# Instance norm over rows of 4096: two of four rows' statistics move to batch-norm instructions and to ScalarE

## The chip, the cores and the metric

The kernel runs on one core of one Trainium2 chip. The metric is the device time of one execution in microseconds (us), input and output in HBM. Lower is better.

## The reference

For each of 256 x 256 = 65,536 rows of 4096 numbers, the mean is taken off and the result is divided by the standard deviation:

```python
x = np.random.randn(256, 256, 4096).astype(np.float32)
eps = np.float32(1e-5)

mean = np.mean(x, axis=2, keepdims=True)
var = np.var(x, axis=2, keepdims=True)
return ((x - mean) / np.sqrt(var + eps)).astype(np.float32)
```

The input is 1073.74 MB and so is the output; each number is read once and written once.

## The kernel before

**Tiles.** The 65,536 rows are cut into 128 tiles. A tile has 128 partitions, and each partition holds K = 4 rows of d = 4096 fp32 numbers, so a tile is 8.39 MB. It lies in one of BUFS = 3 buffers `X[s]` in SBUF and is normalised in place there. One load brings a tile and one store takes it away.

**Order.** Each engine has its program written out by hand, and semaphores tie the programs together. SP issues all loads and stores, from one queue: `store(t)` waits for five counts of `done[s]` and then issues (L157); the `load(t + 2)` that follows in the program waits until `store(t - 1)`, the last from the same buffer, has landed, and then issues (L162). At the start three loads are issued at once. GpSimd only waits for the last stores. On VectorE and ScalarE one tile is handled after the other, in a loop over three tiles (one for each buffer) with a few tiles written out at both ends.

**VectorE**, in `vector_tile`, waits for the load, then

1. sums each of the four rows (`reduce_sum`, L83), and counts `means` up after each;
2. for two rows at a time: waits for ScalarE's roots (`stds`), takes the reciprocal (L91), multiplies it with the negative mean (L93), and normalises the rows in place with `tensor_scalar` (L105), x * rstd + nbias. Of the fourth row it does the last quarter alone, from Q = 3072 on.

**ScalarE**, in `scalar_tile`, follows row by row: when a row's sum is there it takes a Square pass over (sum - d * x) with an accumulated output (L129), which yields the row's squared deviations in `ss`; the squares themselves go to `junk` in PSUM and are never read. After two rows it takes the root of both with one small instruction (L138). At the end of the tile it waits for `scaled` and normalises the first three quarters of the fourth row with an Identity pass (L143).

The waits on an engine's own semaphore (`own_v`, `own_a`) come before an instruction that reads what the engine has just written. `take` waits for a count and clears the semaphore (L67).

Of the kernel before, what the change touches and what calls it, by code (L numbers as in the profile page):

```python
# [9 lines left out]
@with_exitstack  # L10
def kernel(
    ctx: ExitStack,
    tc: tile.TileContext,
    x: bass.AP,
    eps: bass.AP,
    out: bass.AP,
):
    nc = tc.nc
    fp32 = mybir.dt.float32
    AX = mybir.AxisListType  # L20
    AF = mybir.ActivationFunctionType
    ALU = mybir.AluOpType
    P = 128
    K = 4
    BUFS = 3
    Q = 3072

    x_flat = x.flatten_outer_dims()
    out_flat = out.flatten_outer_dims()
    n, d = x_flat.shape  # L30
    assert n % (P * K) == 0 and d & (d - 1) == 0

    ntiles = n // (P * K)
    x_t = x_flat.rearrange("(t p k) d -> t p k d", p=P, k=K)
    out_t = out_flat.rearrange("(t p k) d -> t p k d", p=P, k=K)
    assert ntiles == 128

    pool = ctx.enter_context(tc.tile_pool(name="pool", bufs=1))
    psum = ctx.enter_context(tc.tile_pool(name="psum", bufs=1, space=bass.MemoryType.PSUM))


    eps_tile = pool.tile([P, 1], fp32)

    junk = psum.tile([P, d], fp32)
    X = [pool.tile([P, K, d], fp32, name=f"x{s}") for s in range(BUFS)]
    total, ss, std, rstd, nbias = (
        [pool.tile([P, K], fp32, name=f"{name}{s}") for s in range(BUFS)]
        for name in ("total", "ss", "std", "rstd", "nbias")
    )

    loaded = [nc.alloc_semaphore(f"loaded{s}") for s in range(BUFS)]
    stored = [nc.alloc_semaphore(f"stored{s}") for s in range(BUFS)]
    own_v = nc.alloc_semaphore("own_v")
    own_a = nc.alloc_semaphore("own_a")
    means = nc.alloc_semaphore("means")
    stds = nc.alloc_semaphore("stds")
    scaled = nc.alloc_semaphore("scaled")  # L60
    done = [nc.alloc_semaphore(f"done{s}") for s in range(BUFS)]
    ready = nc.alloc_semaphore("ready")
    issued = nc.alloc_semaphore("issued")

    def take(engine, sem, count):
        engine.wait_ge(sem, count)
        engine.sem_clear(sem)  # L67

    V, A, S, G = nc.vector, nc.scalar, nc.sync, nc.gpsimd

    def vector_tile(s):

        x = X[s]
        own = 0

        def mine(instruction):
            nonlocal own
            own += 1
            return instruction.then_inc(own_v, 1)

        take(V, loaded[s], 16)
        for r in range(K):
            V.reduce_sum(out=total[s][:, r : r + 1], in_=x[:, r, :], axis=AX.X).then_inc(means, 1)  # L83
        for b in range(0, K, 2):
            c = slice(b, b + 2)
            final = b == K - 2
            if final:
                take(V, stds, b // 2 + 1)
            else:
                V.wait_ge(stds, b // 2 + 1)  # L90
            mine(V.reciprocal(out=rstd[s][:, c], in_=std[s][:, c]))  # L91
            V.wait_ge(own_v, own)
            mine(V.scalar_tensor_tensor(  # L93
                out=nbias[s][:, c], in0=total[s][:, c], scalar=-1.0 / d, in1=rstd[s][:, c], op0=ALU.mult, op1=ALU.mult
            ))
            if final:
                take(V, own_v, own)
            else:
                V.wait_ge(own_v, own)
            if final:  # L100
                V.sem_inc(scaled, 1)
            for r in range(b, b + 2):
                c = slice(r, r + 1)
                f = slice(Q, d) if r == K - 1 else slice(0, d)
                V.tensor_scalar(  # L105
                    out=x[:, r, f], in0=x[:, r, f], scalar1=rstd[s][:, c], scalar2=nbias[s][:, c],
                    op0=ALU.mult, op1=ALU.add,
                ).then_inc(done[s], 1)

    def scalar_tile(s):  # L110

        x = X[s]
        last = K - 1
        own = 0

        def mine(instruction):
            nonlocal own
            own += 1
            return instruction.then_inc(own_a, 1)

        for r in range(K):
            c = slice(r, r + 1)
            if own:
                A.wait_ge(own_a, own)
            if r == last:
                take(A, means, K)
            else:
                A.wait_ge(means, r + 1)
            mine(A.activation(  # L129
                out=junk, in_=x[:, r, :], func=AF.Square, bias=total[s][:, c], scale=-float(d), accum_out=ss[s][:, c]  # L130
            ))
            if r % 2:
                c = slice(r - 1, r + 1)
                if r == last:
                    take(A, own_a, own)
                else:
                    A.wait_ge(own_a, own)
                A.activation(  # L138
                    out=std[s][:, c], in_=ss[s][:, c], func=AF.Sqrt, bias=eps_tile, scale=1.0 / d**3
                ).then_inc(stds, 1)  # L140
        c = slice(last, last + 1)
        take(A, scaled, 1)
        A.activation(  # L143
            out=x[:, last, :Q], in_=x[:, last, :Q], func=AF.Identity, bias=nbias[s][:, c], scale=rstd[s][:, c]
        ).then_inc(done[s], 1)

    def rows_of(ap, t):

        if isinstance(t, int):
            return ap[t]  # L150
        first, period, count, i = t
        ap = ap[first : first + period * (count - 1) + 1 : period]
        return ap[bass.ds(i, 1)].rearrange("o p k d -> p (o k) d")

    def store(s, t):
        take(S, done[s], K + 1)
        S.dma_start(out=rows_of(out_t, t), in_=X[s][:, :, :]).then_inc(stored[s], 16)  # L157

    def load(s, t, wait=True):
        if wait:  # L160
            take(S, stored[s], 16)
        S.dma_start(out=X[s][:, :, :], in_=rows_of(x_t, t)).then_inc(loaded[s], 16)  # L162

    last = ntiles - 1
    rounds = (ntiles - 5) // BUFS
    L0 = 2

    with tc.tile_critical():  # L168
        for t in range(BUFS):
            load(t, t, wait=False)  # L170
        store(0, 0)
        store(1, 1)
        load(0, 3)

        with S.Fori(0, rounds) as i:
            for t in range(L0, L0 + BUFS):
                store(t % BUFS, (t, BUFS, rounds, i))
                load((t + 2) % BUFS, (t + 2, BUFS, rounds, i))
        load(last % BUFS, last)
        store((last - 2) % BUFS, last - 2)  # L180
        store((last - 1) % BUFS, last - 1)
        store(last % BUFS, last)
        S.sem_inc(issued, 1)
        take(G, issued, 1)
        for s in range(BUFS):
            take(G, stored[s], 16)

        V.memset(eps_tile, eps).then_inc(ready, 1)  # L188
        vector_tile(0)
        vector_tile(1)  # L190
        with V.Fori(0, rounds) as i:  # L191
            for j in range(BUFS):
                vector_tile((L0 + j) % BUFS)
        vector_tile((last - 2) % BUFS)
        vector_tile((last - 1) % BUFS)
        vector_tile(last % BUFS)

        take(A, ready, 1)
        scalar_tile(0)
        scalar_tile(1)  # L200
        with A.Fori(0, rounds) as i:
            for j in range(BUFS):
                scalar_tile((L0 + j) % BUFS)
        scalar_tile((last - 2) % BUFS)
        scalar_tile((last - 1) % BUFS)
        scalar_tile(last % BUFS)
# [35 lines left out]
```

## Time and profile before

| | us |
|---|---|
| median of three runs | 4962.89 |
| lowest and highest | 4960.41, 4966.53 |
| the profiled execution, its own time | 4962.78 |
| its span, first to last instruction | 4961.0 |
| VectorE busy, 1537 instructions | 3293.7 (66%) |
| ScalarE busy, 1410 instructions | 2401.5 (48%) |
| bytes moved by DMA | 2147.52 MB, mean 433 GB/s |
| load, from issue to landing, median | 50.4 |
| store, from issue to landing, median | 31.6 |

The page and the trace come from one profiled execution. DVE stands for VectorE, ACT for ScalarE, POOL for GpSimd, SP for SyncE; a "q" behind a name is that engine's sequencer. L12 is line 12 of the kernel. The page cuts the span into 40 equal slices and gives each engine's busy share as a digit, in tenths; 9 is 90% or more. Under it stands the mean share of the 16 DMA engines and what they moved. A group of instructions has its line, engine and operation, then output<-input with shapes and the number of instructions; after the first bar the busy time in us and the mean of one in ns, after the second the engine's idle time ahead of them and what ended most of it. A row of the waits reads: who waited for whom, us in all, how many times, the longest. A row of the timeline has the start, the duration, then the group, and in brackets the idle time ahead of it. Several instructions with one name are merged there; "x4 17.40" is four instructions from the first one's start to the last one's end. SP's rows are transfers being issued, not moved.

### The profile page before, as it was taken

How to read it: one execution, taken by the hardware profiler on the slowest of the kernel's cores; microseconds unless marked ns; L12 is line 12 of the kernel's file. 1: busy time of each engine (PE TensorE's matmuls, PEld its weight loads, DVE VectorE, ACT ScalarE, POOL GpSimd, SP SyncE). 2: the span in 40 equal slices, each digit the busy share in tenths (PEclk: the TensorE clock that was granted, in tenths of full speed). 3: DMA queues.
4: the chain of work that ended last, by engine and by line, in shares of the span. 5: the costliest groups of instructions: out<-in, count | busy, mean ns of one | idle time of the engine just before them, and what ended most of it. 6: DMA issues, size and time to landing. Idle time of an engine off the chain costs nothing.

```text
span 4961.0 us, 5413 instructions
## 1 busy us (share of the span) xinstructions
DVE 3293.7 (66%) x1537; ACT 2401.5 (48%) x1410; POOL 0.2 (0%) x4
## 2 busy tenths in 40 slices
DVE  6666666666666666666666666666666666666666
ACT  4454444554445544554445544455444554445544
POOL 0000000000000000000000000000000000000000
DMA  9999999999999999999999999999999999999999
GB/s 423 431 430 435 432 434 435 432 434 436 433 432 438 431 434 435 433 433 436 432 433 434 435 431 434 437 432 433 435 433 433 437 431 434 433 435 432 435 435 414
DMA packets 36866, 2147.52 MB, mean 433 GB/s; under 512 B 4096, under 2 KB 4096, under 8 KB 4096
## 3 DMA queue, kind: packets, MB, share of 16 engines
q1 hardware_dynamic: 36864, 2147.50, 100.0%
q14 instruction: 2, 0.02, 0.0%
HBM read 1073.74 MB, written 1073.74 MB: 433 GB/s over the span
## 4 chain that ended last, share of the span: by engine, by line
DVE 62%; another core or an unknown queue 31%; issue 4%; DMA 2%; DVEq 0%; SPq 0%
DVE total L83 44%; DVE x L105 17%; DMA x<-in_x_dram 1%; DVE nbias L93 1%; DMA out_dram<-x 1%; DVE rstd L91 1%; DVEq L67 0%; DVEq L191 0%; SPq L67 0%; SPq L237 0%; SPq L168 0%
## 5 line engine op out<-in xcount | busy, mean ns | idle before, releaser
L83 DVE TENSOR_REDUCE total<-x 128x1 f32<-128x4096 f32 x512 | 2226.9, 4412 | 1597.4 <-DMA x<-in_x_dram 1597.4
L129 ACT ACTIVATE junk<-x,total 128x4096 f32<-128x4096 f32 x512 | 1882.9, 3678 | 2368.4 <-DVE total L83 2368.3
L105 DVE TENSOR_SCALAR x<-x,rstd,nbias 128x4096 f32<-128x4096 f32 (+1 forms) x512 | 1007.3, 2009 | 33.6 <-DVE nbias L93 28.9
L143 ACT ACTIVATE x<-x,nbias,rstd 128x3072 f32<-128x3072 f32 x128 | 377.3, 2948 | 144.3 <-DVEq L67 144.3
L129 ACT ACTIVATION_READ_ACCUMULATOR junk<-x,total 128x1 f32 x512 | 95.4, 186 | 0.0
L138 ACT ACTIVATE std<-ss,eps_tile 128x2 f32<-128x2 f32 x256 | 75.6, 295 | 19.0
L93 DVE SCALAR_TENSOR_TENSOR nbias<-total,rstd 128x2 f32<-128x2 f32 x256 | 41.0, 160 | 8.9
L91 DVE RECIPROCAL rstd<-std 128x2 f32<-128x2 f32 x256 | 39.8, 156 | 0.0
L129 ACT ACT_TABLE_LOAD x1 | 1.3, 1283 | 1.2 <-DVE eps_tile L188 1.2
L138 ACT ACT_TABLE_LOAD x1 | 1.3, 1283 | 0.0
L188 DVE MEMSET eps_tile<- 128x1 f32 x1 | 0.1, 59 | 1.0 <-SPq L168 1.0
L223 POOL MEMSET const-bfloat16-1.0<- 128x1 bf16 x1 | 0.1, 102 | 0.0
L223 POOL MEMSET const-uint8-127<- 128x1 uint8 x1 | 0.1, 102 | 0.0
L223 POOL MEMSET const-float32-0.0<- 128x1 f32 x1 | 0.1, 99 | 0.2 <-issue 0.2
L223 POOL MEMSET const-float32-1.0<- 128x1 f32 x1 | 0.1, 99 | 0.0
## 6 DMA issues: line engine op xcount, KB each, us to landing
x<-in_x_dram SPq DMA_DIRECT2D x128, 50.4
out_dram<-x SPq DMA_DIRECT2D x128, 31.6
```

Source lines behind the costliest of these rows:

```text
L83: V.reduce_sum(out=total[s][:, r : r + 1], in_=x[:, r, :], axis=AX.X).then_inc(means, 1)
L91: mine(V.reciprocal(out=rstd[s][:, c], in_=std[s][:, c]))
L93: mine(V.scalar_tensor_tensor(out=nbias[s][:, c], in0=total[s][:, c], scalar=-1.0 / d, in1=rstd[s][:, c], op0=ALU.mult, op1=ALU.mult))
L105: V.tensor_scalar(out=x[:, r, f], in0=x[:, r, f], scalar1=rstd[s][:, c], scalar2=nbias[s][:, c], op0=ALU.mult, op1=ALU.add,).then_inc(done ...
L129: mine(A.activation(out=junk, in_=x[:, r, :], func=AF.Square, bias=total[s][:, c], scale=-float(d), accum_out=ss[s][:, c]))
L138: A.activation(out=std[s][:, c], in_=ss[s][:, c], func=AF.Sqrt, bias=eps_tile, scale=1.0 / d**3).then_inc(stds, 1)
L143: A.activation(out=x[:, last, :Q], in_=x[:, last, :Q], func=AF.Identity, bias=nbias[s][:, c], scale=rstd[s][:, c]).then_inc(done[s], 1)
L188: V.memset(eps_tile, eps).then_inc(ready, 1)
L223: nc = _bacc.Bacc("TRN2", target_bir_lowering=False, num_devices=1)
```

## The change

The four rows of a tile are no longer treated alike.

- **Rows 0 and 1**: VectorE sums them as before, ScalarE takes the Square pass.
- **Row 2**: VectorE takes batch-norm statistics in chunks of `F = BN_STATS_FMAX` elements (`bn_stats`) and joins them to mean and variance (`bn_aggr`). ScalarE takes only the root of that variance.
- **Row 3**: ScalarE takes the sum, in an Identity pass with accumulated output, and then the Square pass. A new semaphore `started`, which VectorE counts up when the load has landed, lets ScalarE begin with it at once.
- **Normalising**: VectorE does row 3, row 1 and the first three quarters of row 2; ScalarE does row 0 and the last quarter of row 2. It was three and a quarter rows and three quarters of a row.
- The columns of the small tiles are rotated by one (`column(r)`), so that rows 3 and 0 lie side by side and share a reciprocal and a root. Roots come in three counts of `stds` for a tile instead of two, `means` in three instead of four, `scaled` in two instead of one. `done` stays at five.
- Loads, stores, their order, SP's and GpSimd's programs, tile size and number of buffers stay as they are.

The core of the diff, the unchanged helpers left out:

```diff
+    F = nc.vector.BN_STATS_FMAX
+    chunks = d // F
+    stats = pool.tile([P, chunks, nc.vector.BN_STATS_DIM], fp32)
+    mv = [pool.tile([P, nc.vector.BN_AGGR_DIM], fp32, name=f"mv{s}") for s in range(BUFS)]
+    started = nc.alloc_semaphore("started")
+    def column(r):
+        return (r + 1) % K
...
         take(V, loaded[s], 16)
-        for r in range(K):
-            V.reduce_sum(out=total[s][:, r : r + 1], in_=x[:, r, :], axis=AX.X).then_inc(means, 1)
...
+        V.sem_inc(started, 1)
+        sum_of(0)
+        sum_of(1)
+        for f in range(chunks):
+            part = V.bn_stats(out=stats[:, f, :], in_=x[:, 2, f * F : (f + 1) * F])
+        mine(part)
+        settle()
+        V.bn_aggr(out=mv[s], in_=stats).then_inc(means, 1)
+        V.wait_ge(stds, 1)
+        scales(columns(3, 0))
+        V.sem_inc(scaled, 1)
+        normalise(3, slice(0, d))
+        take(V, stds, 3)
+        c, e = columns(1), columns(2)
+        mine(V.reciprocal(out=rstd[s][:, columns(1, 2)], in_=std[s][:, columns(1, 2)]))
+        settle()
+        mine(V.scalar_tensor_tensor(
+            out=nbias[s][:, c], in0=total[s][:, c], scalar=-1.0 / d, in1=rstd[s][:, c], op0=ALU.mult, op1=ALU.mult
+        ))
+        mine(V.scalar_tensor_tensor(
+            out=nbias[s][:, e], in0=mv[s][:, 0:1], scalar=-1.0, in1=rstd[s][:, e], op0=ALU.mult, op1=ALU.mult
+        ))
+        settle(True)
+        V.sem_inc(scaled, 1)
+        normalise(1, slice(0, d))
+        normalise(2, slice(0, Q))
...
+        take(A, started, 1)
+        mine(A.activation(out=junk, in_=x[:, K - 1, :], func=AF.Identity, accum_out=total[s][:, columns(K - 1)]))
+        A.wait_ge(own_a, own)
+        square(K - 1)
+        A.wait_ge(own_a, own)
+        A.wait_ge(means, 1)
+        square(0)
+        root(columns(3, 0))
+        A.wait_ge(means, 2)
+        square(1)
+        root(columns(1), True)
+        take(A, means, 3)
         A.activation(
-            out=x[:, last, :Q], in_=x[:, last, :Q], func=AF.Identity, bias=nbias[s][:, c], scale=rstd[s][:, c]
-        ).then_inc(done[s], 1)
+            out=std[s][:, columns(2)], in_=mv[s][:, 1:2], func=AF.Sqrt, bias=eps_tile, scale=1.0
+        ).then_inc(stds, 1)
+        A.wait_ge(scaled, 1)
+        normalise(0, slice(0, d))
+        take(A, scaled, 2)
+        normalise(2, slice(Q, d))
```

In the new code `settle` is the wait on `own_v`, `scales` the reciprocal with its multiply, and `normalise` the `tensor_scalar` on VectorE and the Identity pass on ScalarE.

## The prediction

> **What bounds the kernel now.** I read the slices first, because an average can hide a stage; then the DMA section, then the waits, and only then the chain. The page's slices:
>
> ```profile
> DVE  6666666666666666666666666666666666666666
> ACT  4454444554445544554445544455444554445544
> ...
> DMA  9999999999999999999999999999999999999999
> GB/s 423 431 430 435 432 434 435 432 434 436 433 432 438 431 434 435 433 433 436 432 433 434 435 431 434 437 432 433 435 433 433 437 431 434 433 435 432 435 435 414
> ...
> q1 hardware_dynamic: 36864, 2147.50, 100.0%
> ```
>
> VectorE is busy for six tenths of every slice, ScalarE for four or five, and the 16 DMA engines for all of each. The transfers move 431 to 438 GB/s everywhere but in the first slice and the last. There is one queue, filled by SP alone, and what moves (each element in once, out once) is not touched by the change. The waits say the same:
>
> ```profile
> DVE total L83 <- DMA x<-in_x_dram: 1597.4, 125, 21.9
> ```
>
> VectorE spends 1597 us waiting for loads: 125 waits, 12.8 us each. The chain of waits looks different, and here it misleads:
>
> ```profile
> DVE 62%; another core or an unknown queue 31%; issue 4%; DMA 2%; DVEq 0%; SPq 0%
> ```
>
> It is walked back through semaphores: a store was issued because VectorE finished, so VectorE's work gets the blame. The walk does not show that the store, once issued, stood in line behind a load already in the queue. One tile from the middle of the timeline settles that (VectorE and SP; start, duration):
>
> ```profile
> 2406.53 17.40 DVE L83 TENSOR_REDUCE total<-x 128x1 f32<-128x4096 f32 x4 [12.70 <-DMA x<-in_x_dram]
> ...
> 2429.42 3.13 DVE L105 TENSOR_SCALAR x<-x,rstd,nbias 128x4096 f32<-128x4096 f32 x2 [0.19 <-DVE nbias L93]
> ...
> 2432.80 0.34 SPq L157 DMA_DIRECT2D out_dram<-x  x1
> 2433.38 0.35 SPq L162 DMA_DIRECT2D x<-in_x_dram  x1
> 2445.31 17.40 DVE L83 TENSOR_REDUCE total<-x 128x1 f32<-128x4096 f32 x4 [12.76 <-DMA x<-in_x_dram]
> ```
>
> The tile lands at 2406.53 and its store is issued at 2432.80, 26.27 us later. The load of the next tile is still running then and lands at 2445.31. So the store has **12.5 us of cover**: it could come that much later before the DMA engines had nothing to do, and coming earlier only makes it wait longer. Landings are 2445.31 - 2406.53 = 38.78 us apart here; a load and a store of 8.39 MB each at 434 GB/s take 38.66. The period is the transfers' and nothing else.
>
> [...] of the 65,536-byte packets, the median is 2.418 us both where VectorE is busy throughout and where it is idle. So another mix of instructions should not change the rate.
>
> **The change, part by part.** The profiled execution took 4962.78 us, 1.78 around its span of 4961.0; the median of the runs is 4962.89, practically the same. Durations come from these rows:
>
> ```profile
> L83 DVE TENSOR_REDUCE total<-x 128x1 f32<-128x4096 f32 x512 | 2226.9, 4412 | 1597.4 <-DMA x<-in_x_dram 1597.4
> L129 ACT ACTIVATE junk<-x,total 128x4096 f32<-128x4096 f32 x512 | 1882.9, 3678 | 2368.4 <-DVE total L83 2368.3
> L105 DVE TENSOR_SCALAR x<-x,rstd,nbias 128x4096 f32<-128x4096 f32 x384 | 914.8, 2410 | 33.6 <-DVE nbias L93 28.9
> L143 ACT ACTIVATE x<-x,nbias,rstd 128x3072 f32<-128x3072 f32 x128 | 377.3, 2948 | 144.3 <-DVEq L67 144.3
> L105 DVE TENSOR_SCALAR x<-x,rstd,nbias 128x1024 f32<-128x1024 f32 x128 | 103.3, 807 | 0.0
> ```
>
> I follow one tile from its landing (time 0).
>
> VectorE before: 17.40 for four sums (4.33 from start to start), 0.4 to 0.7 of waits and small instructions twice, 4.74 for two rows of normalising, 3.13 for one and a quarter: 26.3.
>
> VectorE after: two sums end at 8.74. The bn_stats (I take the chunk BN_STATS_FMAX as 512 elements, so eight; no view shows it) have no row. [...] 0.69 us each, 5.5 us for eight, an estimate. [...] Ceiling that I allow: twice the estimate, 11. bn_aggr over 8 triples with its wait: 0.2 to 1, I take 0.45. That is 14.7. Reciprocal and multiply (0.156 + 0.160 and the gaps between, 0.4): 15.1. Row 3, 2.41: 17.5. Three small instructions with two waits, 0.8: 18.3. Row 1, 2.37: 20.7. 3072 elements of row 2, interpolated between 807 and 2410 ns, 1.87: **22.5**.
>
> ScalarE after: it starts on the landing, with an Identity pass that sums row 3, at the price of a Square pass (3.68 + 0.19, 3.90 from start to start), then three Squares: 11.7 after the third pass, a root 12.1, the fourth pass 16.0, two roots 16.7. By then the sums (4.4, 8.7) and the aggregate (14.7) are there. Then Identity over row 0, 2.95 plus 1024 elements [...]: 3.8, to 20.5; and a quarter of row 2, 1.2: 21.7. [...]
>
> So the store would be issued at about 22.7 instead of 26.3, **3.6 us earlier**, and its cover grows from 12.5 to 16.1 us. All added work lies beside the transfers, which hide it: value on the path 0. If that cover were gone, the 3.6 us per tile would come through in full.
>
> The new waits: ScalarE now waits for "started" at the head of a tile; nothing is queued behind it but the next tile's work, and VectorE gives it on the landing. VectorE's wait for three roots comes at 17.5, after they are done (16.7). If a wait were late by a microsecond or two, VectorE's last rows and then SP's store would be late by as much, against 16 us of cover. SP's and POOL's programs are unchanged: the same 256 transfers in the same order, five counts per store as before. A load needs the store before the last to have landed; that store was issued near 2394 (38.7 before) and landed about 31.6 later, near 2426, so issuing at about 2429 still finds it done.
>
> **The two ends.** In front: the first store is issued at 49.18, while the third load runs until about 61.6; moved to 45.5 it starts no sooner. At the back: the last store is issued at 4934.63 and stands behind the one before, which by the trace's landing events is complete at 4939.6; issued some 7 us earlier, it still stands behind it. The windows agree (us; VectorE, ScalarE and POOL busy with counts; clock; DMA share; GB/s):
>
> ```profile
> 4920.00:4940.00 20.00, 14.26 (x10) 12.31 (x9) 0.00 (x0) 1.00 1.00 433
> 4940.00:4961.00 21.00, 0.00 (x0) 0.00 (x0) 0.00 (x0) 1.00 0.77 334
> ```
>
> The DMA engines are full to 4940 and then drain; the 0.77 is their emptying at different times, up to the last store's end. Sum: 4962.78 + 0 = 4963; I say 4962.5.
>
> **The rivals.** *Faster, the chain is right:* 3.6 us x 128 = 460 us, 4500 us. Against it stands the queue, full in every slice; at 434 GB/s the 2147.5 MB alone take 4948. What could still come is the removal of small hindrances: landings are on average 38.70 us apart over the middle tiles and 38.59 at the least, from some late packets; 0.11 x 124 = 13 us if all vanished, 4949. Nothing ties them to the old order. Chance 0.04 of more than 0.2%.
>
> *Slower, bn_stats makes VectorE the bound:* its work per tile is on the path once it passes 38.65 us, so once the eight take 5.5 + 16.1 = 21.6 us, 2.7 each, four times my estimate. At five times (3.45 each) a tile is 44.6 us, and 128 x 44.6 + 23 for the first load + 20 for the last store = 5750. No row of before excludes it[...]. Chance 0.03, all slower cases together.
>
> *The change does not do what it says:* the sums could end no earlier because ScalarE is late, leaving the store at 26. The time is the same 4962, so this tells on the trace alone and belongs to no change.
>
> **How the numbers follow.** No change, within 0.2% (10 us, about what a measurement of this kernel can tell from none): 0.93. The three runs lie between 4960.4 and 4966.5; a little more on both sides, for late packets and another few runs, gives 4957 to 4968. The two rivals lie outside with 0.07 together, so the range needs no stretching to them.
>
> **What would show it.** Right: DMA at 9 in all slices near 434 GB/s, VectorE and ScalarE at five tenths or a little more, VectorE's waits for loads up from 12.8 to about 16 us each, store to landing up from 31.6 to about 35, bn_stats near 0.7 us. Wrong: slices with less DMA, VectorE without waits for loads, bn_stats over 2.7 us, or packets whose median leaves 2.418 us.

## The result, and the profile after

The changed kernel takes **4970.27 us** (median of 15 executions, 4968.99 to 4975.68); the kernel before, measured beside it, 4961.23 (15 executions, 4959.56 to 4966.53). The ratio is **1.0018, with a 95% interval of 1.0010 to 1.0025**: slower by 9 us. That is still within the 0.2% that the prediction called no change, but above the top of its range (4968), and the interval does not reach 1.

What the change was to do on the engines, it did. Groups of instructions of the kernel after (busy us, mean ns, idle time ahead), and the wait of VectorE for loads:

```profile
L99 DVE TENSOR_REDUCE total<-x 128x1 f32<-128x4096 f32 x256 | 1119.4, 4414 | 2189.5 <-DMA x<-in_x_dram 2189.5
L121 DVE BATCH_NORM_STATS2 stats<-x 128x6 f32<-128x512 f32 x1024 | 618.9, 678 | 0.0
L124 DVE BATCH_NORM_AGGREGATE mv<-stats 128x2 f32<-128x48 f32 x128 | 47.5, 371 | 4.4
```

```profile
DVE total L99 <- DMA x<-in_x_dram: 2189.5, 125, 32.9
```

A bn_stats over 512 elements takes 678 ns, an aggregate 371, and VectorE waits 2189.5 / 125 = 17.5 us for each load, where it was 12.8. One tile from the middle of the timeline (start, duration; VectorE and SP):

```profile
2408.32 8.75 DVE L99 TENSOR_REDUCE total<-x 128x1 f32<-128x4096 f32 x2 [17.40 <-DMA x<-in_x_dram]
...
2416.98 4.83 DVE L121 BATCH_NORM_STATS2 stats<-x 128x6 f32<-128x512 f32 x8
...
2425.52 4.20 DVE L111 TENSOR_SCALAR x<-x,rstd,nbias 128x4096 f32<-128x4096 f32 x2 [0.19 <-DVE nbias L136]
2429.97 0.34 SPq L205 DMA_DIRECT2D out_dram<-x  x1
2430.55 0.35 SPq L210 DMA_DIRECT2D x<-in_x_dram  x1
2447.09 8.74 DVE L99 TENSOR_REDUCE total<-x 128x1 f32<-128x4096 f32 x2 [17.36 <-DMA x<-in_x_dram]
```

The store is issued 21.65 us after the landing instead of 26.27, and its cover, the time until the load ahead of it has landed, is 17.1 us (2447.09 - 2429.97) instead of 12.5. All this is gain, and all of it is hidden. The loss is in the transfers. The slices of the kernel after:

```profile
DMA  9999999999999999999999999999999999999998
GB/s 422 433 433 433 435 433 436 431 436 433 432 437 432 435 433 432 436 432 435 434 432 436 433 434 434 432 437 432 436 433 433 436 432 436 432 434 435 433 437 380
```

In 39 slices nothing is to be seen; the last has 380 GB/s, where it had 414. The windows of the end show what that is (us; busy time of VectorE, ScalarE and POOL; clock; DMA share; GB/s). First the kernel before, then the one after:

```profile
4950.00:4955.00 5.00, 0.00 (x0) 0.00 (x0) 0.00 (x0) 1.00 0.97 419
4955.00:4961.00 6.00, 0.00 (x0) 0.00 (x0) 0.00 (x0) 1.00 0.13 55
```

```profile
4950.00:4955.00 5.00, 0.00 (x0) 0.00 (x0) 0.00 (x0) 1.00 0.76 328
4955.00:4960.00 5.00, 0.00 (x0) 0.00 (x0) 0.00 (x0) 1.00 0.09 39
4960.00:4965.00 5.00, 0.00 (x0) 0.00 (x0) 0.00 (x0) 1.00 0.06 26
```

A share of 0.06 is 1/16: from 4960 to 4965 **one DMA engine works alone**, at 26 GB/s, while the packets of the other 15 have ended by 4957.4. Before, the share is 0.97 up to 4955, and the last packet of all ends at 4959.5; after, at 4967.1.

That engine had not stopped anywhere. A transfer adds 16 counts to its semaphore (the trace has 4096 for 256 transfers), and there are 16 DMA engines. Each count comes some 0.36 us behind the end of a 4-byte packet, of which there are 4096 too. I take it that each engine gives one, so that the time from the first count to the last is how far the engines have drifted apart. From the trace's landing events, in us, for the landings number 20 to 254 of 256:

```
landing                      20    60   100   140   180   220   254
before                      2.9   4.0   3.7   3.7   4.1   3.5   4.5
after                       3.7   4.1   5.4   7.8  10.2  12.6  14.5
```

Before, the spread settles near 4 us. After, one engine falls back steadily, by 0.12 us a tile. The trace's packet records show how. There are 32,768 packets of 65,536 bytes for 256 transfers and 16 engines, eight for each engine and tile, with a median of 2.418 us. In the middle of the run after, the packets of the other engines have that duration to within 3 ns, but for a few late ones; those of the last engine take longer, a little in each (ns over 2418, means over the 15 stores and 15 loads among landings 150 to 180):

```
the eight packets of a store   10.7  4.1  1.0  6.5 13.9 21.6 34.7 24.5    sum 117
the eight packets of a load     0.9  0.2  4.0  1.9  4.9  2.0  5.6  2.0    sum  21
```

Five sixths are lost in stores, which this engine moves during the first 19.3 us after a landing, and most of it from 9 us on, when bn_stats, roots and normalising run. The kernel before has the same at a smaller size: one engine, the last one from about landing 222 on, loses 52 ns in a store and 23 in a load. The question of the experiments was therefore: what of the change reaches one DMA engine?

### The profile page after: what moved, and what is told of

Its sections match the earlier page's. It is cut to its first block, busy times and chain, and to the rows that moved or that the text cites. A ratio compares the mean times of both kernels' runs of the same rounds, so it can differ in the third digit from the quotient of the medians.

```text
span 4968.7 us, 6565 instructions
## 1 busy us (share of the span) xinstructions
DVE 2684.0 (54%) x2433; ACT 2639.5 (53%) x1666; POOL 0.2 (0%) x4
## 2 busy tenths in 40 slices
DMA packets 36867, 2147.52 MB, mean 432 GB/s; under 512 B 4096, under 2 KB 4096, under 8 KB 4096
## 4 chain that ended last, share of the span: by engine, by line
DVE 50%; another core or an unknown queue 43%; issue 4%; DMA 2%; ACT 0%; DVEq 0%; SPq 0%; ACTq 0%
DVE total L99 22%; DVE x L111 13%; DVE stats L121 12%; DMA x<-in_x_dram 1%; DVE mv L124 1%; DMA out_dram<-x 1%; DVE nbias L104 0%; DVE rstd L131 0%; DVE nbias L133 0%; DVE nbias L136 0%; DVEq L72 0%; ACT junk L156 0%; DVE rstd L102 0%; ACT junk L176 0%
## 5 line engine op out<-in xcount | busy, mean ns | idle before, releaser
L99 DVE TENSOR_REDUCE total<-x 128x1 f32<-128x4096 f32 x256 | 1119.4, 4414 | 2189.5 <-DMA x<-in_x_dram 2189.5
L176 ACT ACTIVATE junk<-x 128x4096 f32<-128x4096 f32 x128 | 459.1, 3587 | 2241.9 <-DVEq L72 2241.9
L156 ACT ACTIVATE junk<-x,total 128x4096 f32<-128x4096 f32 x384 | 1409.9, 3672 | 8.3
L111 DVE TENSOR_SCALAR x<-x,rstd,nbias 128x4096 f32<-128x4096 f32 (+1 forms) x384 | 846.5, 2232 | 43.2 <-DVE nbias L136 23.9
L171 ACT ACTIVATE x<-x,nbias,rstd 128x4096 f32<-128x4096 f32 (+1 forms) x256 | 629.6, 2506 | 0.0
L121 DVE BATCH_NORM_STATS2 stats<-x 128x6 f32<-128x512 f32 x1024 | 618.9, 678 | 0.0
L165 ACT ACTIVATE std<-ss,eps_tile 128x2 f32<-128x2 f32 (+1 forms) x256 | 75.5, 295 | 19.0
L124 DVE BATCH_NORM_AGGREGATE mv<-stats 128x2 f32<-128x48 f32 x128 | 47.5, 371 | 4.4
L187 ACT ACTIVATE std<-mv,eps_tile 128x1 f32<-128x1 f32 x128 | 35.7, 279 | 0.0
L176 ACT ACTIVATION_READ_ACCUMULATOR junk<-x 128x1 f32 x128 | 23.9, 186 | 0.0
L176 ACT ACT_TABLE_LOAD x1 | 1.3, 1283 | 23.1 <-DVEq L72 23.1
L165 ACT ACT_TABLE_LOAD x1 | 1.3, 1283 | 0.0
## 6 DMA issues: line engine op xcount, KB each, us to landing
out_dram<-x SPq DMA_DIRECT2D x128, 36.4
```

Of the source, the lines that this page charges most:

```text
L99: V.reduce_sum(out=total[s][:, columns(r)], in_=x[:, r, :], axis=AX.X).then_inc(means, 1)
L111: V.tensor_scalar(out=x[:, r, f], in0=x[:, r, f], scalar1=rstd[s][:, c], scalar2=nbias[s][:, c], op0=ALU.mult, op1=ALU.add,).then_inc(done ...
L121: part = V.bn_stats(out=stats[:, f, :], in_=x[:, 2, f * F : (f + 1) * F])
L124: V.bn_aggr(out=mv[s], in_=stats).then_inc(means, 1)
L156: mine(A.activation(out=junk, in_=x[:, r, :], func=AF.Square, bias=total[s][:, c], scale=-float(d), accum_out=ss[s][:, c]))
L165: A.activation(out=std[s][:, c], in_=ss[s][:, c], func=AF.Sqrt, bias=eps_tile, scale=1.0 / d**3).then_inc(stds, 1)
```

## The experiments

Each was timed against the kernel before on the same chip; the kernel before had medians of 4960.8 to 4961.1 in all four groups. "Lost per store" is the sum over the eight packets of the engine that falls behind, a mean over the stores in which that engine is clearly the last one (by 40 ns or more) and none of its packets is late by 90 ns or more. In the kernel before these are ten stores near the end.

### First group: bn_stats, the number of instructions, or the earlier store?

**e1_bn_added**: the kernel before with

```diff
             V.reduce_sum(out=total[s][:, r : r + 1], in_=x[:, r, :], axis=AX.X).then_inc(means, 1)
+        for f in range(d // F):
+            V.bn_stats(out=spare[:, f, :], in_=x[:, 2, f * F : (f + 1) * F])
```

> The kernel before, plus eight bn_stats over row 2 on VectorE after the four sums of each tile; what they write is not used. The changed kernel was 9 us slower and its trace ends with one DMA engine working alone for some 8 us. Theory A (each VectorE instruction that is fetched takes about 10 ns of one of the 16 DMA engines, whatever it does): eight more per tile, 8 x 10 ns x 128 = 10 us, about 4971 us, and in the trace one DMA engine alone at the end (DMA share 0.06). Theory B (bn_stats alone disturbs a DMA engine): about 4971 us as well. Theory C (the earlier store or ScalarE's new order is the cause): no change, 4961 us, since both are as before here.

Measured: 5010.15 us (4973 to 5027), ratio 1.0091 (1.0061 to 1.0122). Far more than any of the theories said.

**e2_sums_added**: the same place and count with another operation.

```diff
+        for f in range(d // F):
+            V.reduce_sum(out=spare[:, f : f + 1], in_=x[:, 2, f * F : (f + 1) * F], axis=AX.X)
```

> The kernel before, plus eight reduce_sum of 512 elements each over row 2 after the four sums of each tile; their output is not used. The same count, operand and length as eight bn_stats. Theory A (the count of VectorE's instructions): about 4971 us and one DMA engine alone at the end. Theory B (bn_stats alone): 4961 us. Theory C (earlier store or ScalarE's order): 4961 us.

Measured: 4995.54 us (4973 to 5022), ratio 1.0061 (1.0033 to 1.0090). Plain sums do much the same as bn_stats. For theory B, bn_stats alone, that decides less than it seems to, for e7 will show that both lose for a reason of their own.

**e3_tiny_added**:

```diff
+        for f in range(8):
+            V.memset(spare[:, f : f + 1], 0.0)
```

> The kernel before, plus eight memsets of 128x1 on VectorE after the four sums of each tile, not used. Next to no data is read, and the eight take about half a microsecond. Theory A (count of instructions): about 4971 us. Theory B (bn_stats alone) and theory C (store or ScalarE's order): 4961 us. A variant of A, that reading 4096 elements twice is what counts: 4961 us here and 4971 with eight added sums.

Measured: 4961.82 us (4961 to 4964), ratio 1.0000 (0.9992 to 1.0009). No loss in time, so theory A falls in the form in which it was put (10 ns for each instruction, wherever). The trace keeps something of it: late in the run one engine loses 68 ns per store, 44 of them in the last packet, where the eight memsets lie; in the kernel before it is 52, with 29 in the last packet. That is 16 ns for eight memsets, 2 ns each. For most of the run others stood behind that engine, so its loss sets the end only by the last microsecond or so.

**e4_after_no_bn**: the changed kernel, with

```diff
-        for f in range(chunks):
-            part = V.bn_stats(out=stats[:, f, :], in_=x[:, 2, f * F : (f + 1) * F])
-        mine(part)
-        settle()
-        V.bn_aggr(out=mv[s], in_=stats).then_inc(means, 1)
+        V.reduce_sum(out=mv[s][:, 0:1], in_=x[:, 2, :], axis=AX.X).then_inc(means, 1)
...
-            out=std[s][:, columns(2)], in_=mv[s][:, 1:2], func=AF.Sqrt, bias=eps_tile, scale=1.0
+            out=std[s][:, columns(2)], in_=ss[s][:, columns(1)], func=AF.Sqrt, bias=eps_tile, scale=1.0
```

> The changed kernel with the eight bn_stats and the bn_aggr replaced by one reduce_sum over row 2; row 2's scale and bias are then made from stand-ins (its raw sum, and row 1's squares), so row 2 is not normalised rightly. Nine VectorE instructions become one; ScalarE's order, the semaphores and the early store stay (store to landing about 36 us). Theory A and theory B: back to about 4961 to 4962 us. Theory C: stays at 4970 us.

Measured: 4967.53 us (4966 to 4981), ratio 1.0013 (1.0007 to 1.0020). It lies between the theories: 2 to 3 of the 9 us go with the eight bn_stats and the bn_aggr, 6 to 7 stay. Lost per store: 92 ns. Theory B falls here: most of the loss needs no bn_stats.

e1 and e2 have one thing in common that e3 has not: their store comes 5 us later. That makes two questions of one.

### Second group: cover on one side, the stretch of the store on the other

**e7_one_sum_added**: the kernel before with a single late instruction.

```diff
+        V.reduce_sum(out=spare, in_=x[:, 2, :], axis=AX.X)
```

> The kernel before, plus one reduce_sum over 4096 elements (not used) after the four sums. One instruction, 4.4 us: the store is issued about 30.6 us after the landing, 8 us before the load ahead of it has landed. It separates the two things that eight added sums (4996 us) and eight added bn_stats (5010 us) had in common. If the lost cover made them slow (about 7 us left, and late packets on many DMA engines at once): 4985 to 5010 us. If it was the number of instructions that read SBUF: 4961 to 4963 us.

Measured: 5006.65 us (4974 to 5021), ratio 1.0084 (1.0059 to 1.0108). One instruction of 4.4 us costs as much as eight bn_stats, so **it is the lost cover that makes e1 and e2 slow**, though VectorE still waits for every load. The timeline of e7:

```profile
2413.78 0.34 SPq L159 DMA_DIRECT2D out_dram<-x  x1
2414.36 0.35 SPq L164 DMA_DIRECT2D x<-in_x_dram  x1
2421.97 17.40 DVE L84 TENSOR_REDUCE total<-x 128x1 f32<-128x4096 f32 x4 [8.34 <-DMA x<-in_x_dram]
```

Cover is 2421.97 - 2413.78 = 8.2 us. In the middle of the run the engines stay 6.1 us apart, and 13 packets a tile are late by 60 ns or more, 411 on average, against 2.5 of 219 before: 13 x 411 / 16 = 334 ns for each engine and tile, 43 us over 128 tiles (4 before), so most of the 46 us. Cover is counted for the last engine. The one in front is done 6.1 us sooner, so its next packets were issued only 2 us ahead, and one bunch of late packets lies just there, 31 to 35 us after the landing. In e1 and e2, with about 8 us of cover too, the spread stands at 5.3 to 6.6 us. Why a second bunch comes 9 to 13 us after the landing was not settled, nor what makes so many packets late at once.

**e5_sums_split**: the changed kernel, with rows 0 and 1 summed in chunks.

```diff
-            V.reduce_sum(out=total[s][:, columns(r)], in_=x[:, r, :], axis=AX.X).then_inc(means, 1)
+            for f in range(chunks):
+                part = V.reduce_sum(out=parts[:, r, f : f + 1], in_=x[:, r, f * F : (f + 1) * F], axis=AX.X)
+            mine(part)
+            settle()
+            V.reduce_sum(out=total[s][:, columns(r)], in_=parts[:, r, :], axis=AX.X).then_inc(means, 1)
```

> The changed kernel, with the sums of rows 0 and 1 each made from eight reduce_sum of 512 elements and one over the eight parts: 18 VectorE instructions in place of two, all within the first 11 us after the landing, while the 16 DMA engines move a store; about 1.5 us more per tile, still 14 us of cover. Theory D (one DMA engine's store packets are slowed by each instruction that VectorE and ScalarE issue while a store is moving; in the changed kernel's trace that engine loses 115 ns per store and 30 per load, all others 0): 16 more at 3 to 5 ns is 50 to 80 ns a tile, 6 to 10 us, about 4977 us. Theory E (it is writing to SBUF in that stretch, the earlier normalising, that slows it): 4970 us. Theory F (cover alone sets how far one engine may fall behind): 4969 us or less.

Measured: 4970.02 us (4968 to 4973), ratio 1.0017 (1.0011 to 1.0024). Theory D, at 3 to 5 ns an instruction, missed by 7 us. Lost per store is 130 ns until the spread reaches 13.5 us, against 115 in the changed kernel, and next to nothing in loads, where the changed kernel loses 23.

**e6_after_delayed**: the changed kernel, started later.

```diff
-        V.sem_inc(started, 1)
+        V.reduce_sum(out=spare, in_=x[:, 3, :], axis=AX.X).then_inc(started, 1)
```

> The changed kernel, with one more reduce_sum over 4096 elements (not used) at the head of each tile before ScalarE is let go: both engines start 4.4 us later, the store is issued about 26 us after the landing as in the kernel before, and the last 4 us of the small instructions and of the normalising move out of the store's stretch into the load's. Theory D and theory E: the engine that falls behind loses some 50 ns a tile less, 4963 to 4966 us. Theory F: less cover, so it may fall behind less, about 4963 too. Were bn_stats or ScalarE's order as such to blame: 4970 us.

Measured: 4964.03 us (4962 to 4978), ratio 1.0008 (1.0000 to 1.0016). **With 4.4 us more work in each tile it is 6 us faster than the changed kernel.** Lost per store: 66 ns. bn_stats, ScalarE's new order and every instruction of the change are still there; only where they lie against the store is different, and the cover, which is that of the kernel before. The smaller cover (theory F) is not what holds the loss down: the engines here stay 6.9 us apart for most of the run, and with the same cover e11 below comes to 10.7.

**e8_junk_sbuf**: the kernel before, with

```diff
-    junk = psum.tile([P, d], fp32)
+    junk = pool.tile([P, d], mybir.dt.bfloat16)
```

> The kernel before, with the Square passes' unused output in SBUF (bf16, 8 KB per partition) instead of PSUM: ScalarE then writes to SBUF during most of a store, with the same instructions. Theory E (writes to SBUF by the engines slow a store): slower, 4966 us or more. Theory D (the number of instructions in that stretch): 4961 us.

Measured: 4960.90 us (4960 to 4997), ratio 1.0005 (0.9994 to 1.0016): no change. Theory E has nothing for it here. Lost per store: 51 ns, as in the kernel before.

### Third group: which operation in the time of the store?

**e9_scale_early**: as e6, but the delay is made of normalising.

```diff
+        V.tensor_scalar(out=x[:, 0, :], in0=x[:, 0, :], scalar1=1.0, scalar2=0.0, op0=ALU.mult, op1=ALU.add)
+        mine(V.tensor_scalar(out=x[:, 1, :], in0=x[:, 1, :], scalar1=1.0, scalar2=0.0, op0=ALU.mult, op1=ALU.add))
+        settle()
         V.sem_inc(started, 1)
```

> The changed kernel, delayed at the head of each tile by two tensor_scalar in place over rows 0 and 1 (times 1.0 plus 0.0, which changes nothing) before ScalarE is let go: 4.7 us, like the 4.4 us of the delay by one more reduce_sum, which ran at 4964 us. Only the operation in the first 5 us of a store differs. Theory G (the in-place normalising by VectorE, when it falls into the time of a store, slows one DMA engine's packets, 30 to 40 ns for each 2.4 us of it; in the kernel before it lies nearly all in the time of a load): two more are 60 to 80 ns a tile, 8 to 10 us, about 4972 us. If something else in the stretch from 14 to 19 us after the landing is at fault (small instructions, roots, ScalarE): about 4964 us.

Measured: 4963.89 us (4963 to 4975), ratio 1.0007 (0.9999 to 1.0015), as e6. Theory G falls.

**e10_scalar_early**: as e6, with ScalarE writing to SBUF in the first 4 us.

```diff
+        V.reduce_sum(out=spare, in_=x[:, 2, :], axis=AX.X)
...
+        mine(A.activation(out=x[:, 3, :], in_=x[:, 3, :], func=AF.Identity, scale=1.0))
+        A.wait_ge(own_a, own)
```

> The changed kernel, with an Identity pass in place over row 3 on ScalarE (times 1.0, changes nothing) at the head of each tile, while VectorE takes one more reduce_sum over row 2 (not used): both engines are 3.9 to 4.4 us later, as in the delayed kernel that ran at 4964 us, but ScalarE writes fp32 to SBUF in the first 4 us of a store. Theory H (ScalarE's normalising in the time of a store slows one DMA engine): about 30 to 60 ns a tile, 4968 to 4972 us. Theory G (only VectorE's does): 4964 us.

Measured: 4965.61 us (4963 to 4981), ratio 1.0013 (1.0006 to 1.0019); lost per store 71 ns. It is 1.6 us above e6 and below theory H's 4968: at most a small part.

So it is none of the operations that were tried. I then counted, over the traces, the instructions that end on VectorE and ScalarE within 19.3 us of a landing (waits and branches too), plus all semaphore updates in that time, and set both beside the loss:

```
kernel      instructions + updates in a store   lost per store   time
before               18 + 27                      52 ns          4961
e3                   26 + 27                      68             4961.8
e6                   25 + 29                      66             4964.0
e10                  30 + 31                      71             4965.6
e4                   31 + 40                      92             4967.5
after                38 + 40                     115             4970.3
e5                   54 + 42                     130             4970.0
```

From 45 events to 78 the loss grows by 63 ns, some 1.9 ns for each. e5 falls short of that: its 18 further events cost 15 ns, not 34, and its loads lose nothing. A count that fits afterwards is no proof; the last group puts it to the test.

### Last group: events put there on purpose

**e12_tiny_in_load** and **e13_tiny_in_store** are the changed kernel with the same lines in two places: behind the last `normalise` of the tile, and behind `sum_of(1)`.

```diff
+        for f in range(32):
+            V.memset(spare[:, f : f + 1], 0.0)
```

> The changed kernel, plus 32 memsets of 128x1 on VectorE behind the last normalising of each tile, 22 to 24 us after the landing, while the DMA engines move a load; the store does not wait for them. Theory K with its second half (events in the time of a load cost nothing): 4970 us as without them. If events cost the same in a load: 32 x 2.5 ns x 128 = 10 us more, 4980 us. Not the count at all: 4970 us.

> The changed kernel, plus the same 32 memsets of 128x1 on VectorE, placed after the two sums of each tile, 9 to 11 us after the landing, while the DMA engines move a store; about 2 us later store, 14 us of cover. Theory K: 32 x 2.5 ns x 128 = 10 us more, about 4980 us, less what the delay of 2 us takes off (some 2 us by the run that was delayed by 4.4). Were the number of events not the cause: 4967 to 4969 us, from the delay alone.

Measured: in the load 4971.49 us (4969 to 4984), ratio 1.0023 (1.0015 to 1.0031), next to the changed kernel's 1.0018; in the store **4984.81 us** (4981 to 4988), ratio 1.0046 (1.0033 to 1.0060). Lost per store: 113 ns in e12, as without the memsets; 189 in e13, until its engines are as far apart as they get. One tile of each, from the landing to the memsets, e12 first:

```profile
2407.91 8.74 DVE L100 TENSOR_REDUCE total<-x 128x1 f32<-128x4096 f32 x2 [16.93 <-DMA x<-in_x_dram]
...
2429.27 0.49 DVE L145 MEMSET spare<- 128x1 f32 x32
```

```profile
2414.53 8.75 DVE L100 TENSOR_REDUCE total<-x 128x1 f32<-128x4096 f32 x2 [17.01 <-DMA x<-in_x_dram]
...
2423.22 0.44 DVE L122 MEMSET spare<- 128x1 f32 x31
```

In e12 they lie 21.4 us behind the landing, when the last engine too is at a load; in e13 8.7 us, in the midst of the store. The packets show the place (ns over 2418, after and e12 over landings 120 to 150, e13 over 90 to 120):

```
after  10.5  3.9  1.7  5.3  7.6 22.5 40.8 22.2
e12    10.4  4.3  1.8  5.3 11.1 21.1 35.9 22.9
e13     9.2  5.2  2.7 49.7 46.6 14.0 39.4 22.1
```

The memsets of e13 take half a microsecond for all 32 (not 2 us, as I had written), where the fourth packet ends and the fifth begins. Those two grow, by 83 ns for 32 instructions: 2.6 ns each. These memsets count no semaphore, so the end of an instruction alone is enough.

**e11_pool_busy**: the kernel before, with GpSimd busy at something that nothing uses.

```diff
+        with G.Fori(0, 512) as i:
+            for _ in range(16):
+                G.memset(spare, 0.0).then_inc(own_g, 1)
+                take(G, own_g, 1)
```

> The kernel before, with 8192 small memsets (128x256) on GpSimd from the start of the kernel on, each with a semaphore that GpSimd alone waits for; nothing else uses them, and they should end within the first half of the run. Theory K (every instruction and semaphore update that ends on any engine while a store moves takes 2 to 3 ns from one DMA engine): at two or three memsets and as many updates per us, 80 or more events in each store, one DMA engine loses 150 ns or more per tile while they last and little afterwards, so some 10 to 15 us for the whole, about 4972 us, unless that engine was ahead at first. If only VectorE and ScalarE matter: 4961 to 4963 us.

Measured: **5001.76 us** (5000 to 5008), ratio 1.0088 (1.0074 to 1.0101), some four times the loss that was expected. The memsets lasted longer than I had thought, to 4580 us and not half the run. Their group, and a window of the end:

```profile
L188 POOL MEMSET spare<- 128x256 f32 x8192 | 3272.9, 400 | 1309.2 <-POOL spare L188 240.0
```

```profile
4995.00:5000.00 5.00, 0.00 (x0) 0.00 (x0) 0.00 (x0) 1.00 0.06 26
```

One memset every (3272.9 + 1309.2) / 8192 = 0.56 us is 35 memsets in a store. With each goes the instruction that clears its semaphore, and two updates, the count and the clearing. By the trace that makes, with the loop's own, 82 instructions of GpSimd and 74 updates more in a store. The last engine loses about 340 ns per store, spread over all eight packets (some 25 to 75 each), and at the end it works alone again. That is 288 ns more than before for 156 events, 1.8 ns each. VectorE's and ScalarE's programs, the order of transfers and the cover (12.5 us) are those of the kernel before. In these executions, then, **what ends on an engine, not what it does for the work, takes time from one DMA engine while that one stores.**

In three of the runs the drift came to a limit. In e7, e11 and e13 the spread stands still at 6.1, 10.7 and 14.7 us, with a cover of 8.3, 12.5 and 16.8 (medians over the run): each time about 2 us less. After that the engines in front run out of work and wait for the last: in e11, from 1500 to 3500 us, 15 packets a tile are late by 60 ns or more, 360 on average, which is some 340 ns for each engine and tile, as much as the last one loses in its stores. The changed kernel came to 14.5 us, with 17.1 of cover, only at its very end.

## Why the prediction was wrong, point by point

- **What bounds the kernel: right.** The transfers set the period in both kernels (landings 38.78 us apart in the tile shown of before, 38.77 after), and a store 4.6 us earlier brought nothing. (The third slice has 430 GB/s, not 431 or more as the prediction says; nothing rests on it.)
- **The sum for the engines: right, a little pessimistic.** Store at 22.7 predicted, 21.65 measured; cover 16.1 and 17.1; bn_stats 0.69 and 0.678 (4.83 for eight, as starts overlap, not 5.5); VectorE's wait about 16 and 17.5; store to landing about 35 and 36.4; two table loads in the whole run, of 1283 ns each, as before, though Square, Sqrt and Identity alternate in every tile. The 0.69 us for bn_stats was the author's estimate, which no row of the kernel before shows; the 678 ns bear it out. The 3.8 us for ScalarE's Identity over a row and the 1.2 for a quarter of one were estimates too, measured at 3.79 and 1.23, and so was the 0.45 for the aggregate with its wait: the instruction alone takes 0.37 (it reads 128x48, six numbers from each of eight bn_stats, not three). At the back the last store came 1.5 us earlier (4933.09), not 7, and stood behind the one before all the same.
- **The step that failed: "another mix of instructions should not change the rate", and with it "value on the path 0".** That compute instructions leave a DMA alone was not shown; what the traces gave for it was the packets' median, 2.418 us with VectorE busy and idle. In e11 and e13 instructions that the work does not need do slow a DMA engine, by 288 ns more per store than before and by 74 more than after (189 - 115); where the two meet was not measured. A median was the wrong view: what counts is the slowest of 16 engines, which in the changed kernel loses 1 to 35 ns in a store's packet of 2418. The term put at nothing is the 33 further events in a store: 115 - 52 = 63 ns for each of 128 tiles, 8 us by this estimate, where 9 were measured.
- **The tail was seen and not asked.** The prediction read 0.77 in the last window as the engines' "emptying at different times" and let it be. How different, and who is last, is the part of this time that a kernel can change.
- **The range** was made from the spread of three runs and from late packets. No unknown effect on the transfers' own rate was in it, so its top was 2 us too low. That the time still came within 0.2% was luck: the term was not weighed, and e13's 32 small instructions more would have broken it.
- **The rival on the slower side had the wrong price.** It let VectorE's work grow until no cover was left, 38.65 us a tile. e7 lost 46 us with 8.2 us of cover left, so bn_stats at 1.7 us each (8.8 us more for eight, which leaves 8.3 of the 17.1) would by that, as an estimate, already have cost as much; 2.7 was not the point from which it decides. That 2.7 would have been 5.3 ns for each of 512 elements, where the sums of the kernel before have 1.08 (4412 / 4096) and bn_stats came to 1.32 (678 / 512).
- **"The chain is right"** was rightly given little: VectorE's share of it fell from 62% to 50%, and the time rose.

What is shown: events in the time of a store slow one DMA engine (33 more of them, 63 ns more per store), those in the time of a load hardly (113 ns with e12's 32 memsets, 115 without), and the change moves many into the store's time. What is not: by which way the end of an instruction reaches a DMA engine, which engine it is, and why e5 is partly spared. One rival stands untested: the events counted are the very ones of which the recording keeps an entry each (6565 instructions and 8647 semaphore updates in the trace of the kernel after), and every execution came with its recorded span. Whether recording them is what takes the time, so that an execution without it would lose nothing, was not tried. No version here beats the kernel before; the nearest of the changed kernel's kind, e6 and e9, are 3 us behind it.

## What to carry to other kernels

When transfers bound a kernel, ask which of the DMA engines ends last: look at the last microseconds for a share near 1/16, and at the time from a landing's first count to its last. Work that is hidden is not always free: on a path with nothing to gain, more and shorter instructions, or the same ones moved into the time of the stores, cost a few parts in a thousand here (1.8 in the changed kernel, 4.6 in e13), at least in executions that are recorded as these were. And cover should be counted for the engine in front, not for the landing: here 12.5 us was enough and 8.2 was not.

## What the runs showed of the hardware that was not expected

- An instruction or semaphore update that ended during a store took about 2 ns from one of 16 DMA engines (1.8 in e11, 1.9 from before to after, 2.6 in e13, less in e5); 32 memsets in half a microsecond cost it 83 ns in e13, the same 32 in a load (e12) nothing that could be seen: 113 ns per store with them, 115 without. Whether the recording has a part in this is open.
- 8192 memsets on GpSimd, without any part in the work, slowed a kernel bound by transfers by 41 us of 4961 (e11).
- One instruction of 4.4 us more in each tile, with VectorE still waiting 8 us for its load, cost 46 us (e7).
- The 16 engines drifted apart by as much as the cover less about 2 us: 6.1, 10.7 and 14.7 us with 8.3, 12.5 and 16.8 of cover (e7, e11, e13).
